# The second FFN's last product as seven half products (Strassen's scheme) instead of one full product

## The chip, the cores and the metric

One core of a Trainium2 chip runs the whole kernel. The metric is the device time of one execution in microseconds (us), as the median of several executions. The core has a matmul engine (TensorE, PE in the profile, with its weight loads as PEld), a vector engine (VectorE, DVE), an activation engine (ScalarE, ACT), a general engine (GpSimd, POOL) and a queue engine for transfers (SyncE, SP). ACT and POOL can start transfers too. Each engine takes its own instructions in order, and semaphores tie the engines together. TensorE writes its sums into PSUM, eight banks of 128 x 512 floats; everything else lives in SBUF (128 partitions) or in device memory (DRAM).

## What is computed

The reference is a residual block: a first feed-forward network (FFN), two token mixers side by side, a second FFN and a last normalisation. There are 512 tokens, 1024 model columns and 2816 hidden columns. What matters here is the end of it:

```
def swiglu(h, w1, w3, w2):
    return (jax.nn.silu(h @ w1) * (h @ w3)) @ w2

x = x + 0.5 * swiglu(rms_norm(x, ffn2_norm[l]), ffn2_w1[l], ffn2_w3[l], ffn2_w2[l])
return rms_norm(x, final_norm)
```

The "last product" of the title is the `@ w2` of the second FFN: hidden values (512 tokens x 2816) times `ffn2_w2` (2816 x 1024). Half of its result is added to x, and each token's row is then normalised by its root mean square.

## The kernel before

All large products are made to float32 accuracy from three passes in a reduced format. A float32 tile is split into a high part (a cast) and a low part (the tile less its high part); `mm3` (line 121) issues three matmuls, high x high, high x low and low x high, into one PSUM bank. `split_w` (line 111) casts on ACT (line 114) and subtracts on DVE (line 115); `split` (line 138) does the same for other tiles (lines 140 and 141).

The model columns are the partitions of the activations nearly everywhere: `xT[c]` holds columns 128c to 128c + 127 of x as 128 partitions x 512 tokens. `Norm.scale` (line 162) makes the split of the scaled x, tiles `xh` and `xl`, eight of each.

`ffn` (line 447) runs two stages. The first goes over 22 blocks j of 128 hidden columns. For each, 24 matmuls with `w1` fill the bank `pa` and 24 with `w3` the bank `pb`; `hidden` (line 452) scales both by the token's 1/rms, applies SiLU and multiplies, and splits the result into `hh[j]` and `hl[j]`. The weights come as 512 KB transfers on SP's queue into three rotating buffers `raw`, and go through `load_w`. The second stage makes the product with `w2`.

In the second FFN this second stage has two forms. Columns 0 to 511 of the result (m = 0 to 3) have model columns as the output's partitions: weights are the stationary operand, the hidden values of all tokens move, 22 x 3 matmuls for each m into the bank `pd`. The result is added to `xT[m]` (line 499), and `almost` squares it for the row sums and turns it over by four transposes (`tokens`, line 1124) into O, which has tokens as partitions. Columns 512 to 1023 are made by `last` (line 1158) with tokens as the output's partitions: 128 tokens of hidden values are stationary, 512 columns of weights move, 22 x 3 matmuls for each of four token blocks into the banks `po`. `hold` (line 1148) brings eight of the 22 weight blocks early into the tiles of `xh` and `xl` (`own`), which are free by then. Eight small matmuls (`os`, line 1163) add up the squares of the first half. The end (lines 1182 to 1191), once for each token block, adds the residual, squares, forms 1/rms, scales both halves and stores them, one on ACT's and one on SP's queue.

A scheduler puts each engine's instructions in order when the program is built, from its own estimate of times; on the chip that order is fixed.

Of the kernel before, what the change touches and what calls it, by code (L numbers as in the profile page):

```python
# [9 lines left out]
F32 = mybir.dt.float32  # L10
# [40 lines left out]
def kernel(  # L51
# [18 lines left out]
    def bank(name, pool_=None):  # L70
        pool_ = pool_ or pm
        return pool_.tile([P, T], F32, tag="b", name=name)

    def tmp(name, shape=(P, T), dt=F32, tag="t", **kw):
        return tp.tile(list(shape), dt, tag=tag, name=name, **kw)
# [42 lines left out]
    def load_w(aps, kt, n, eng=None):  # L118
        return split_w(load_raw(aps, kt, n), kt, n, eng)

    def mm3(ps, whi, wlo, xhi, xlo, first, last):
        pe.matmul(ps, whi, xhi, start=first, stop=False)  # L122
        pe.matmul(ps, whi, xlo, start=False, stop=False)  # L123
        return pe.matmul(ps, wlo, xhi, start=False, stop=last)  # L124

    def ln_act(out, in_, **kw):
        pre = act.preload_act_table_set("natural_log_exp_and_others")
# [23 lines left out]
    rtp = xctx.enter_context(tc.tile_pool(name="xr1", bufs=1, side="right"))  # L151
    xT = [rtp.tile([P, T], F32, name=f"xT{c}") for c in range(KD)]

    class Norm:


# [5 lines left out]
        def scale(s, c, eng=None, src=None):  # L162
            g = pc(s.gain + c)
            src = xT[c][:] if src is None else src
            hi = xp.tile([P, T], F32R, tag=f"xh{c}", name=f"xh{c}")
            lo = xp.tile([P, T], F32R, tag=f"xl{c}", name=f"xl{c}")
            if eng is act:
                act.activation(hi[:], src, AF.Copy, scale=g)
            else:
                dve.tensor_scalar(hi[:], src, g, None, op0=ALU.mult)  # L170
            dve.scalar_tensor_tensor(lo[:], src, g, hi[:].bitcast(F32),
                                     op0=ALU.mult, op1=ALU.subtract)
            s.hi[c], s.lo[c] = hi, lo
# [71 lines left out]
    with tc.tile_pool(name="x0", bufs=1) as x0:  # L245
# [22 lines left out]
                qpe.transpose(xps[c][:, b * P:(b + 1) * P], xin[c][:, b, :], ident[:])  # L268

        def x_hi(c):  # L270
            nrm.hi[c] = xp.tile([P, T], F32R, tag=f"xh{c}", name=f"xh{c}")
            from_ = (xps if c < 2 else xT)[c][:]
            if c % 2:
                qact.activation(nrm.hi[c][:], from_, AF.Copy, scale=pc(PAR_FFN1 + c))
            else:
                qdve.tensor_scalar(nrm.hi[c][:], from_, pc(PAR_FFN1 + c), None, op0=ALU.mult)

        def x_lo(c):
            nrm.lo[c] = xp.tile([P, T], F32R, tag=f"xl{c}", name=f"xl{c}")
            from_ = (xps if c < 2 else xT)[c][:]  # L280
            qdve.scalar_tensor_tensor(nrm.lo[c][:], from_, pc(PAR_FFN1 + c), f32(nrm.hi[c][:]),
                                      op0=ALU.mult, op1=ALU.subtract)
# [161 lines left out]
        pool.tensor_copy(ux[q1], loraw[q1, :])  # L444
        pool.tensor_tensor(ux[q1], loraw[q1, :], f32(ux[q1]), op=ALU.subtract)

    def ffn(nrm, w1, w3, w2, nxt, during=(), first=None, final=None):
        with tc.tile_pool(name="hp", bufs=1) as hp:
            hh, hl = [], []
            hp.tile([P, 96], F32, name="lead")  # L450

            def hidden(j, pa, pb):
                a = tmp("fa")
                dve.tensor_tensor(a[:], pa[:], nrm.rstd[:], op=ALU.mult)  # L454
                sa = tmp("fs")
                act.activation(sa[:], a[:], AF.Silu)
                b = tmp("fb")
                dve.tensor_tensor(b[:], pb[:], nrm.rstd[:], op=ALU.mult)  # L458
                h = tmp("fh")
                dve.tensor_tensor(h[:], b[:], sa[:], op=ALU.mult)  # L460
                hi = hp.tile([P, T], F32R, name=f"hh{j}")
                lo = hp.tile([P, T], F32R, name=f"hl{j}")
                split(hi[:], lo[:], h[:], "dve")
                hh.append(hi)
                hl.append(lo)

            summed = None
            for j in range(KF):
# [18 lines left out]
                if j in during:  # L487
                    with tc.issue_after(pin.ins), tc.issue_after(loads[-1].ins):
                        during[j]()
                hidden(j, pa, pb)  # L490
            cuts = ((0, 8), (8, 8), (16, 6))

            for m in range(KD // 2 if final else KD):
                ps = bank("pd")
                for k0, kn in cuts:
                    wh, wl = load_w([(0, w2[0][k0 * P:(k0 + kn) * P, m * P:(m + 1) * P])], kn, P)
                    for k in range(k0, k0 + kn):
                        mm3(ps[:], wh[:, k - k0, :], wl[:, k - k0, :], hh[k][:], hl[k][:], k == 0, k == KF - 1)
                dve.scalar_tensor_tensor(xT[m][:], ps[:], 0.5, xT[m][:], op0=ALU.mult, op1=ALU.add)
                nxt(m)  # L500
                if final and m == 1:
                    held = final[0]()
            if final:
                final[1](hh, hl, held)

    mix = Norm(PAR_MIX)
    xsave = dp.tile([KD, P, T], F32, name="xsave")
# [13 lines left out]
    with ExitStack() as mx:  # L521
# [567 lines left out]
        for m in range(3):  # L1089
            late_tanh(m, parted)  # L1090
        rtp = ctx.enter_context(tc.tile_pool(name="xr2", bufs=1, side="right"))
        xT[:] = [rtp.tile([P, T], F32, name=f"xS{c}") for c in range(KD)]
        for c in range(KD):
            nc.gpsimd.dma_start(xT[c][:], xsave[c])
        ms = []
# [21 lines left out]
    fg = fp.tile([P, D], F32, name="fg")  # L1117
    nc.gpsimd.dma_start(fg[:], final_norm.unsqueeze(0).broadcast_to([P, D]))
    O = fp.tile([P, NB, D], F32, name="O")
    acc = fp.tile([P, T], F32, name="facc")  # L1120
    ss, cb = [fp.tile([P, NB], F32, name=n) for n in ("ss", "cb")]
    fr = fp.tile([P, NB], F32, name="fr")

    def tokens(m, scaled=True):
        ps = pr.tile([P, NB, P], F32, tag="b", name="ot")
        for b in range(NB):
            pe.transpose(ps[:, b, :], xT[m][:, b * P:(b + 1) * P], ident[:])
        o, ms_ = O[:, :, m * P:(m + 1) * P], slice(m * P, (m + 1) * P)
        if scaled:
            dve.tensor_tensor(o, ps[:], fg[:, ms_].unsqueeze(1).broadcast_to([P, NB, P]), op=ALU.mult)  # L1130
        else:
            act.copy(o, ps[:])

    def almost(m):
        if m == 0:
            tc.keep_in_program_order(act.preload_act_table_set("natural_log_exp_and_others"))
            act.activation(acc[:], xT[m][:], AF.Square)
        else:
            sq = tmp("osq")
            act.activation(sq[:], xT[m][:], AF.Square)  # L1140
            pool.tensor_tensor(acc[:], acc[:], sq[:], op=ALU.add)
        tokens(m)


    HC = slice(D // 2, D)
    KS = 10

    def hold():
        ws = {}
        for k in range(KS, KS + KD, 2):  # L1150
            raw = load_raw([(0, ffn2_w2[0][k * P:(k + 2) * P, HC])], 2, 512)
            for i in range(2):
                parts = [xp.tile([P, T], F32R, tag=f"x{n}{k - KS + i}", name=f"own{n}{k + i}") for n in "hl"]
                split(parts[0][:], parts[1][:], raw[:, i, :])
                ws[k + i] = [t[:] for t in parts]
        return ws

    def last(hh, hl, ws):
        for m in range(KD // 2, KD):
            tokens(m, False)  # L1160
        os = bank("os", pf)
        for b in range(NB):
            pe.matmul(os[:, b:b + 1], acc[:, b * P:(b + 1) * P], ones[:, 0:1], start=True, stop=True)
        dve.tensor_scalar(cb[:], os[:, 0:NB], 1.0 / D, RMS_EPS, op0=ALU.mult, op1=ALU.add)
        ps = [bank(f"po{b}", q_) for b, q_ in zip(range(NB), (pm, pm, pf, pf))]

        def some(b, ks):
            bs = slice(b * P, (b + 1) * P)
            for k in ks:
                mm3(ps[b][:], hh[k][:, bs], hl[k][:, bs], *ws[k], k == 0, k == KF - 1)  # L1170

        for k in [*range(0, KS, 2), *range(KS + KD, KF, 2)]:
            wh, wl = load_w([(0, ffn2_w2[0][k * P:(k + 2) * P, HC])], 2, 512)
            for i in range(2):
                ws[k + i] = wh[:, i, :], wl[:, i, :]
            if k < KS:
                for b in range(NB):
                    some(b, (k, k + 1))
        for b in range(NB):
            some(b, range(KS, KF))  # L1180
            lo_, hi_, r = O[:, b, 0:D // 2], O[:, b, HC], fr[:, b:b + 1]
            dve.scalar_tensor_tensor(hi_, ps[b][:], 0.5, hi_, op0=ALU.mult, op1=ALU.add)
            junk = tmp("osq")
            act.activation(junk[:], hi_, AF.Square, accum_out=ss[:, b:b + 1])
            act.activation(r, ss[:, b:b + 1], AF.Ln, bias=cb[:, b:b + 1], scale=1.0 / D)
            act.activation(r, r, AF.Exp, scale=-0.5)
            dve.scalar_tensor_tensor(hi_, hi_, r, fg[:, HC], op0=ALU.mult, op1=ALU.mult)
            act.activation(lo_, lo_, AF.Copy, scale=r)
            bs = slice(b * P, (b + 1) * P)
            nc.scalar.dma_start(out[0, bs, 0:D // 2], lo_)  # L1190
            nc.sync.dma_start(out[0, bs, HC], hi_)

    ffn(nrm2, ffn2_w1, ffn2_w3, ffn2_w2, almost, final=(hold, last))


_INS = ['x', 'ffn1_norm', 'ffn1_w1', 'ffn1_w3', 'ffn1_w2', 'mix_norm', 'w_in', 'shift_mu',
# [21 lines left out]
```

## Time and profile before

| | |
|---|---|
| median of three executions | 1181.81 us (1181.7 to 1183.05) |
| the profiled execution | 1182.64 us, of which its span is 1180.9 us |
| granted TensorE clock, mean | 0.997 |
| transfers | 122.52 MB, mean 104 GB/s |
| POOL's (software) queue | 12.06 MB, 3.2% of 16 transfer engines |
| stage of the hidden values, second FFN | 809 to 1049 us of the span |
| its last product | 1049 to 1174 us |
| end after the last matmul | to 1180.9 us |

The span is what the profiler saw of one execution; the execution's own time is 1.7 us longer. Rows that group instructions give source line, engine, operation, the tile written and the tiles read, the shape, the count, then the busy time in us, the mean duration of one in ns, and the idle time of the engine just before them with what ended it. Rows of a timeline begin with the start in us and the duration in us. TensorE's matmuls overlap each other, so their busy times add up to more than the time that they take.

### The profile page before, as it was taken

How to read it: one execution, taken by the hardware profiler on the slowest of the kernel's cores; microseconds unless marked ns; L12 is line 12 of the kernel's file. 1: busy time of each engine (PE TensorE's matmuls, PEld its weight loads, DVE VectorE, ACT ScalarE, POOL GpSimd, SP SyncE). 2: the span in 40 equal slices, each digit the busy share in tenths (PEclk: the TensorE clock that was granted, in tenths of full speed). 3: DMA queues.
4: the chain of work that ended last, by engine and by line, in shares of the span. 5: the costliest groups of instructions: out<-in, count | busy, mean ns of one | idle time of the engine just before them, and what ended most of it. 6: DMA issues, size and time to landing. Idle time of an engine off the chain costs nothing.

```text
span 1180.9 us, 15709 instructions
## 1 busy us (share of the span) xinstructions
PE 1165.0 (99%) x6264; PEld 945.6 (80%) x6264; DVE 656.3 (56%) x981; ACT 459.5 (39%) x746; POOL 87.4 (7%) x138
## 2 busy tenths in 40 slices
PE   9999999999999999999999999999999999999997
PEld 7888888888887888887677776778888888888886
DVE  6745444543444697686767666766545445544221
ACT  6322222222224765346786765424222222223222
POOL 1200000001111111401000020121000000000100
PEclk9999999999999999999999999999999999999999
DMA  6333333323334343344123244633333333325211
GB/s 179 112 107 89 98 99 94 103 81 115 116 116 113 86 114 113 112 138 116 37 64 88 79 125 126 205 93 105 89 107 90 93 104 92 105 81 169 90 36 71
DMA packets 201783, 122.52 MB, mean 104 GB/s; under 512 B 9934, under 2 KB 191246, under 8 KB 201710
## 3 DMA queue, kind: packets, MB, share of 16 engines
q1 hardware_dynamic: 195134, 107.62, 31.6%
q0 software_dynamic: 3760, 12.06, 3.2%
q10 hardware_dynamic: 2816, 1.84, 0.5%
q8 instruction: 49, 0.80, 0.3%
q14 instruction: 24, 0.20, 0.1%
HBM read 110.82 MB, written 10.68 MB: 103 GB/s over the span
## 4 chain that ended last, share of the span: by engine, by line
PE 91%; ACT 3%; DVE 3%; DMA 2%; issue 1%; SPq 0%; ACTq 0%; DVEq 0%
PE pb L124 7%; PE pb L122 7%; PE pb L123 7%; PE pa L124 6%; PE pa L122 6%; PE pa L123 6%; PE pd L124 5%; PE pd L123 5%; PE pd L122 5%; PE pgt L122 3%; PE pgt L124 2%; PE pgt L123 2%; PE pk L123 2%; PE pk L122 2%; PE pk L124 2%; PE po L122 2%
## 5 line engine op out<-in xcount | busy, mean ns | idle before, releaser
L114 ACT CAST whi<-raw 128x1024 fp32r<-128x1024 f32 (+3 forms) x193 | 192.8, 1000 | 586.1 <-PE pa L123 177.8
L115 DVE TENSOR_TENSOR wlo<-raw,whi 128x1024 fp32r<-128x1024 f32 (+3 forms) x193 | 224.2, 1162 | 122.8 <-ACT whi L114 122.7
L124 PE MATMUL pb<-xh,wlo 128*128 128x512 f32 x344 | 133.9, 389 | 0.1
L124 PE MATMUL pa<-xh,wlo 128*128 128x512 f32 x344 | 133.9, 389 | 0.0
L122 PE MATMUL pb<-xh,whi 128*128 128x512 f32 x344 | 133.8, 389 | 0.0
L123 PE MATMUL pb<-xl,whi 128*128 128x512 f32 x344 | 133.8, 389 | 0.0
L123 PE MATMUL pa<-xl,whi 128*128 128x512 f32 x344 | 133.8, 389 | 0.0
L122 PE MATMUL pa<-xh,whi 128*128 128x512 f32 x344 | 133.8, 389 | 0.0
L458 DVE TENSOR_TENSOR fb<-pb,rstd 128x512 f32<-128x512 f32 x43 | 29.7, 691 | 139.5 <-PE pb L124 139.5
L124 PE MATMUL pd<-hh,wlo 128*128 128x512 f32 x264 | 103.1, 391 | 0.5 <-DVE wlo L115 0.5
L122 PE MATMUL pd<-hh,whi 128*128 128x512 f32 x264 | 102.8, 389 | 0.0
L123 PE MATMUL pd<-hl,whi 128*128 128x512 f32 x264 | 102.8, 389 | 0.0
L124 PEld LDWEIGHTS pb<-xh,wlo 128*128 128x128 f32 x344 | 64.5, 188 | 13.9 <-DVE wlo L241 0.6
L124 PEld LDWEIGHTS pa<-xh,wlo 128*128 128x128 f32 x344 | 64.6, 188 | 13.5
L123 PEld LDWEIGHTS pb<-xl,whi 128*128 128x128 f32 x344 | 64.6, 188 | 13.5
L123 PEld LDWEIGHTS pa<-xl,whi 128*128 128x128 f32 x344 | 64.5, 188 | 13.5
L122 PEld LDWEIGHTS pb<-xh,whi 128*128 128x128 f32 x344 | 64.6, 188 | 13.3
L122 PEld LDWEIGHTS pa<-xh,whi 128*128 128x128 f32 x344 | 64.6, 188 | 13.3
L454 DVE TENSOR_TENSOR fa<-pa,rstd 128x512 f32<-128x512 f32 x43 | 29.7, 691 | 70.3 <-PE pa L124 70.2
L124 PEld LDWEIGHTS pd<-hh,wlo 128*128 128x128 f32 x264 | 49.6, 188 | 11.1 <-DVE wlo L115 0.9
L123 PEld LDWEIGHTS pd<-hl,whi 128*128 128x128 f32 x264 | 49.6, 188 | 10.4
L122 PEld LDWEIGHTS pd<-hh,whi 128*128 128x128 f32 x264 | 49.6, 188 | 10.2
(395 smaller groups left out, 2026.0 us busy)
## 6 DMA issues: line engine op xcount, KB each, us to landing
raw<-in_ffn_w_dram SPq DMA_DIRECT2D x121, 512.0 KB
raw<-in_w_in_dram SPq DMA_DIRECT2D x40, 512.0 KB
raw<-in_ffn_w_dram SPq DMA_DIRECT2D x12, 384.0 KB
raw<-in_w_out_dram SPq DMA_DIRECT2D x8, 512.0 KB
gsave<-gs SPq DMA_DIRECT2D x9, 256.0 KB
xin<-in_x_dram SPq DMA_DIRECT2D x8, 256.0 KB
xsave<-xT POOLq DMA_DIRECT2D x8, 256.0 KB, 2.3
G<-gsave POOLq DMA_DIRECT2D x8, 256.0 KB, 3.0
```

The lines of the kernel that those rows point to most:

```text
L114: (hi_eng or act).copy(hi[:], raw[:])
L115: (eng or dve).tensor_tensor(lo[:], raw[:], hi[:].bitcast(F32), op=ALU.subtract)
L122: pe.matmul(ps, whi, xhi, start=first, stop=False)
L123: pe.matmul(ps, whi, xlo, start=False, stop=False)
L124: return pe.matmul(ps, wlo, xhi, start=False, stop=last)
L454: dve.tensor_tensor(a[:], pa[:], nrm.rstd[:], op=ALU.mult)
L458: dve.tensor_tensor(b[:], pb[:], nrm.rstd[:], op=ALU.mult)
```

## The change

The last product of the second FFN is made by Strassen's scheme in Winograd's form. The hidden columns are cut into two halves of 11 blocks, the tokens into two halves of 256, and the columns of w2 into two halves of 512. Seven products of such halves replace eight. Each has 11 k steps, two blocks of 128 tokens as stationary operands and 512 columns of weights moving, three matmuls each. Fifteen sums of halves are needed:

- On the side of the hidden values DVE makes four sums (`second`, `rest`) of float32 tiles, before the split; `hidden` therefore stores unsplit values, and `operand` splits a group of four blocks x 256 tokens at once, by ACT and DVE.
- On the side of w2, four sums are made by transfers. `load` issues for products 1, 2, 3 and 5 a transfer on POOL's queue with `accum_op=ALU.add`, which adds a quarter of w2 from DRAM onto what lies in SBUF; for products 0, 4 and 6 a plain transfer on SP's queue. A product's weights are six pieces, five of 128 x 2 x 512 floats and one half of that. Each piece has one buffer `sum[g]` and one pair of split tiles `slots[g]`. `weight` splits a piece and then issues the transfer for the next product's piece into the same buffer.
- On the side of the result, PSUM banks X, Y and Z go on collecting over several products, and DVE adds them, with factors of 0.5 and -0.5, into O (`out`).

All of O's residual is turned over beforehand: `begin`, which runs beside steps 1 to 8 of the stage of hidden values, transposes `xT[m]` into O and starts the first plain transfers into the space of `xT`. For that the tiles of `xT`, `xh` and `xl` are allotted in pairs. Row sums of squares now come from ACT over O; the eight small matmuls and `almost` go.

```
+        def load(s, n, g):
+            r, c, more = ((0, 0, 0), (0, 1, 1), (1, 1, 1), (1, 0, 1), (1, 1, 0), (0, 1, 1), (1, 0, 0))[n]
+            k0, k1 = r * KH + 2 * g, r * KH + min(2 * g + 2, KH)
+            src = s.w[k0 * P:k1 * P, c * (D // 2):(c + 1) * (D // 2)].rearrange("(k p) c -> p k c", p=P)
+            if more:
+                nc.gpsimd.dma_start(s.sum[g], src, accum_op=ALU.add)
+            else:
+                nc.sync.dma_start(s.sum[g], src)
+
+        def weight(s, n, g):
+            split(*s.slots[g], s.sum[g])
+            if n < 6:
+                s.load(n + 1, g)
...
+        def second(s, g):
+            d = s.lo[g][:, :, TH:]
+            dve.tensor_tensor(d, d, s.hi[g][:, :, TH:], op=ALU.subtract)
+            s.operand(1, g)
+
+        def rest(s, g):
+            a11, d = s.lo[g][:, :, 0:TH], s.lo[g][:, :, TH:]
+            a12, a22 = s.hi[g][:, :, 0:TH], s.hi[g][:, :, TH:]
+            dve.tensor_tensor(d, d, a11, op=ALU.subtract)
+            dve.tensor_tensor(s.e[g], a12, d, op=ALU.add)
+            dve.scalar_tensor_tensor(a11, d, -1.0, a22, op0=ALU.mult, op1=ALU.subtract)
+
+        def operand(s, n, g):
+            q, lo, hi = s.q[n % 2][g], s.lo[g], s.hi[g]
+            a, z = slice(0, TH), slice(TH, T)
+            split(q[:, 0], q[:, 1], (lo[:, :, a], lo[:, :, z], lo[:, :, z], hi[:, :, z], n == 4 and s.e[g], lo[:, :, a], hi[:, :, a])[n])
...
+            def mm(ps, n, i, k, fresh):
+                q, c = s.q[n % 2][k // 4][:, :, k % 4], slice(i * P, (i + 1) * P)
+                wh, wl = [t[:, k % 2] for t in s.slots[k // 2]]
+                mm3(ps[i][:], q[:, 0, c], q[:, 1, c], wh, wl, fresh and k == 0, k == KH - 1, n in (2, 4, 5))
...
+            put(0, 3, s.second, 2)
+            put(0, 8, s.rest, 2)
+            for n in range(6):
+                for g in range(6):
+                    put(n, 2 * g + (5 if n == 0 else 3), s.weight, n + 1, g)
+                for g in range(3):
+                    if n + 2 < 7:
+                        put(n, min(4 * g + 3, 10) + (4 if n == 0 else 0), s.operand, n + 2, g)
+            for n, ps in enumerate((X, Y, X, Z, Y, X)):
+                for k in range(KH):
+                    for i in range(2):
+                        mm(ps, n, i, k, n in (0, 1, 3))
+                    for f, *a in after.get((n, k), ()):
+                        f(*a)
+                for i in range(2):
+                    for b, cols, by in (((0, LO, 0.5),), ((2, HI, 0.5),), ((0, HI, -0.5),), ((2, LO, 0.5),),
+                                        ((0, HI, 0.5),), ((2, LO, 0.5), (2, HI, -0.5)))[n]:
+                        s.out(ps[i][:], b + i, cols, by)
```

The seventh product (into V) runs the first six k steps for both token blocks and then the other five for one block after the other, so that the first block's end can begin earlier. The end of each token block (`part`, `whole`) has the same steps as before.

More of the change, by code (lines that the diff above doesn't have):

```diff
@@ L119, in load_w, with mm3 @@
         return split_w(load_raw(aps, kt, n), kt, n, eng)
[L121 to L124, printed above, removed]
+    def mm3(ps, whi, wlo, xhi, xlo, first, last, onto=False):
+        pe.matmul(ps, whi, xhi, start=first, stop=False, skip_group_check=onto)
+        pe.matmul(ps, whi, xlo, start=False, stop=False, skip_group_check=onto)
+        return pe.matmul(ps, wlo, xhi, start=False, stop=last, skip_group_check=onto)
     def ln_act(out, in_, **kw):
@@ L152, with pair @@
     xT = [rtp.tile([P, T], F32, name=f"xT{c}") for c in range(KD)]
+    pairs = {}
+    def pair(n, c):
+        if c % 2 == 0:
+            pairs[n, c // 2] = xp.tile([P, 2, T], F32R, tag=f"x{n}{c // 2}", name=f"x{n}{c}")
+        return pairs[n, c // 2][:, c % 2]
     class Norm:
@@ L164, in scale @@
             src = xT[c][:] if src is None else src
-            hi = xp.tile([P, T], F32R, tag=f"xh{c}", name=f"xh{c}")
-            lo = xp.tile([P, T], F32R, tag=f"xl{c}", name=f"xl{c}")
+            hi, lo = pair("h", c), pair("l", c)
             if eng is act:
@@ L270, in x_hi @@
         def x_hi(c):
-            nrm.hi[c] = xp.tile([P, T], F32R, tag=f"xh{c}", name=f"xh{c}")
+            nrm.hi[c] = pair("h", c)
             from_ = (xps if c < 2 else xT)[c][:]
@@ L278, in x_lo @@
         def x_lo(c):
-            nrm.lo[c] = xp.tile([P, T], F32R, tag=f"xl{c}", name=f"xl{c}")
+            nrm.lo[c] = pair("l", c)
             from_ = (xps if c < 2 else xT)[c][:]
@@ L445, in place_params, with ffn @@
         pool.tensor_tensor(ux[q1], loraw[q1, :], f32(ux[q1]), op=ALU.subtract)
-    def ffn(nrm, w1, w3, w2, nxt, during=(), first=None, final=None):
+    def ffn(nrm, w1, w3, w2, nxt, during=(), first=None, seven=None, beside=()):
         with tc.tile_pool(name="hp", bufs=1) as hp:
@@ L450, in ffn @@
             hp.tile([P, 96], F32, name="lead")
+            if seven:
+                seven = seven(hp, w2[0])
             def hidden(j, pa, pb):
@@ L458, in hidden @@
                 dve.tensor_tensor(b[:], pb[:], nrm.rstd[:], op=ALU.mult)
+                if seven:
+                    dve.tensor_tensor(seven.hidden(j), b[:], sa[:], op=ALU.mult)
+                    seven.ready(j)
+                    return
                 h = tmp("fh")
@@ L489, in ffn @@
                         during[j]()
+                if j in beside:
+                    beside[j]()
+                if seven and j == KF - 1:
+                    seven.places()
                 hidden(j, pa, pb)
+            if seven:
+                seven.run()
+                return
             cuts = ((0, 8), (8, 8), (16, 6))
-            for m in range(KD // 2 if final else KD):
+            for m in range(KD):
                 ps = bank("pd")
@@ L500, in ffn @@
                 nxt(m)
[L501 to L504, printed above, removed]
     mix = Norm(PAR_MIX)
@@ L1091 @@
         rtp = ctx.enter_context(tc.tile_pool(name="xr2", bufs=1, side="right"))
-        xT[:] = [rtp.tile([P, T], F32, name=f"xS{c}") for c in range(KD)]
+        xS = [rtp.tile([P, 2, T], F32, name=f"xS{c}") for c in range(KD // 2)]
+        xT[:] = [xS[c // 2][:, c % 2] for c in range(KD)]
         for c in range(KD):
@@ L1119, with tokens @@
     O = fp.tile([P, NB, D], F32, name="O")
[L1120 to L1124, printed above, removed]
+    third = fp.tile([P, 2, T], F32, name="third")
+    ss, ss2, cb, fr = [fp.tile([P, NB], F32, name=n) for n in ("ss", "ss2", "cb", "fr")]
+    def tokens(m):
         ps = pr.tile([P, NB, P], F32, tag="b", name="ot")
@@ L1127, in tokens @@
             pe.transpose(ps[:, b, :], xT[m][:, b * P:(b + 1) * P], ident[:])
[L1128 to L1135, printed above, removed]
-            tc.keep_in_program_order(act.preload_act_table_set("natural_log_exp_and_others"))
[L1137 to L1142, printed above, removed]
@@ L1145 @@
[L1145 to L1151, printed above, removed]
-            for i in range(2):
[L1153 to L1191, printed above, removed]
@@ L1196, with seven @@
+    box = []
+    def seven(hp, w):
+        box.append(Seven(hp, w))
+        return box[0]
+    ffn(nrm2, ffn2_w1, ffn2_w3, ffn2_w2, None, seven=seven,
+        beside={1 + m: (lambda m=m: box[0].begin(m)) for m in range(KD)})
 _INS = ['x', 'ffn1_norm', 'ffn1_w1', 'ffn1_w3', 'ffn1_w2', 'mix_norm', 'w_in', 'shift_mu',
```

90 lines of the change are left out of this document (89 added, 1 removed).

## The prediction

> **What bounds the kernel now.** I read the shares of the page first, then the chain that ended last.
>
> ```profile
> PE 1165.0 (99%) x6264; PEld 945.6 (80%) x6264; DVE 656.3 (56%) x981; ACT 459.5 (39%) x746; POOL 87.4 (7%) x138
> PE 91%; ACT 3%; DVE 3%; DMA 2%; issue 1%; SPq 0%; ACTq 0%; DVEq 0%
> ```
>
> TensorE holds 91% of the chain, so a matmul that goes away is worth its place in the row of matmuls, if nothing else becomes late. That place is not its duration. The timeline of TensorE, as the last product begins:
>
> ```profile
> 1048.97 0.39 PE L122 MATMUL pd<-hh,whi 128*128 128x512 f32 x1
> 1049.19 0.39 PE L123 MATMUL pd<-hl,whi 128*128 128x512 f32 x1
> ...
> 1059.85 0.39 PE L122 MATMUL pd<-hh,whi 128*128 128x512 f32 x1
> ```
>
> Each lasts 0.39 us, but the next starts 0.22 to 0.23 us later. Line 122 opens each k, and 1059.85 is the opening of k = 16: 48 matmuls in 10.88 us, 0.2267 us each. The stage's other marks, from views of single tiles and of time:
>
> ```profile
> L124 PE MATMUL po<-whi,hl x56: 388/389/398, 1111.5 to 1173.8; 128*128 128x512 f32 x56
> ...
> 1117.88 0.28 PE L1163 MATMUL os<-onesr,facc 128*128 128x1 f32 x2
> 1118.02 1.07 PE L1127 MATMUL ot<-ident,xS 128*128 128x128 f32 x8
> 1118.93 0.73 PE L1163 MATMUL os<-onesr,facc 128*128 128x1 f32 x6
> 1119.52 0.47 PE L122 MATMUL po<-whi,hh 128*128 128x512 f32 x1
> ...
> 1080.48 0.50 PE L124 MATMUL pd<-hh,wlo 128*128 128x512 f32 x1 [0.47 <-DVE wlo L115]
> ```
>
> The last matmul starts at 1173.8, so the stage's place on TensorE runs from 1048.97 to about 1174.05, 125.1 us. Its 528 matmuls (4 column blocks x 22 x 3, then 22 x 4 token blocks x 3) fill 528 x 0.2267 = 119.7 us. The other 5.4 us: 32 transposes at 0.91/8 = 0.114 us, 3.65 us; eight row-sum matmuls, 1.64 - 0.91 = 0.73 us; a stall of 0.47 us; 0.5 us of small waits.
>
> **The change part by part.** *Matmuls.* Seven products of 11 k x 2 token blocks x 3 are 462 instead of 528: 66 x 0.2267 = 14.96 us less, same shape. One product is 66 too, so it lasts 14.96 us. The row-sum matmuls go, 0.73 us, and the stall and the small waits have no counterpart I can name: 1.0 us.
>
> *Transposes.* All 32 move ahead, into the stage that makes the hidden values. TensorE has no hole there:
>
> ```profile
> 814.70:1048.70 234.00, 234.00 (x1034) 193.73 (x1033) 116.69 (x149) 61.06 (x69) 0.00 (x0) 1.00 0.33 96
> ```
>
> The columns are length, PE, PEld, DVE, ACT and POOL busy, granted clock, DMA share and GB/s. So they cost 3.65 us there and save 3.65 us later: nothing. DVE has room, 117 of 234 us, and loses two instructions in each of 22 steps (rows below, 0.42 + 0.69 us). In return each half-group of hidden values is split at once, and twice a burst of five (one difference, its split, three sums, 5 x 1.22 = 6.1 us) meets the step's 2 x 1.22 + 3 x 0.69 = 4.5 us: 10.6 us in a step of 48 x 0.2267 = 10.88 us. It fits barely; I take 0 and keep 2 us as its upper end.
>
> *Splits.* Durations by form:
>
> ```profile
> L115 DVE TENSOR_TENSOR wlo<-raw,whi 128x1024 fp32r<-128x1024 f32 x58 | 70.9, 1222 | 39.8 <-ACT whi L114 39.8
> L114 ACT CAST whi<-raw 128x1024 fp32r<-128x1024 f32 x58 | 61.1, 1054 | 218.9 <-PE pa L123 91.2 <-PE pb L123 81.9 <-PE pd L123 22.5
> L141 DVE TENSOR_TENSOR hl<-fh,hh 128x512 fp32r<-128x512 f32 x22 | 15.2, 693 | 0.8
> L140 DVE CAST hh<-fh 128x512 fp32r<-128x512 f32 x22 | 9.2, 419 | 0.0
> L140 ACT CAST ownh<-raw 128x512 fp32r<-128x512 f32 x8 | 4.6, 618 | 6.2 <-DMA raw<-in_ffn_w_dram 6.2
> L115 DVE TENSOR_TENSOR wlo<-raw,whi 128x768 fp32r<-128x768 f32 x4 | 3.8, 955 | 2.4 <-ACT whi L114 2.4
> L114 ACT CAST whi<-raw 128x768 fp32r<-128x768 f32 x4 | 3.3, 836 | 12.2 <-PE pd L123 8.3 <-issue 3.9
> L1182 DVE SCALAR_TENSOR_TENSOR O<-po,O 128x512 f32<-128x512 f32 x4 | 2.8, 692 | 21.8 <-PE po L124 21.8
> ```
>
> Per product DVE subtracts five weight pieces of 128x1024 and a half one, three token operands (two of 1024, one of 768 columns) and adds two results to O: 5 x 1.22 + 0.69 + 2 x 1.22 + 0.96 + 2 x 0.69 = 11.6 us of 14.96. ACT casts the same: 5 x 1.05 + 0.62 + 2 x 1.05 + 0.84 = 8.8 us. Both are hidden while TensorE sets the pace: 0 us; without that cover DVE would be the floor at 11.6 us a product.
>
> *Weight sums.* This is the unknown. Products 1, 2, 3 and 5 take sums that 24 adding transfers on POOL's queue make in SBUF (20 of 512 KB, 4 of 256 KB); products 0, 4 and 6 load plainly on SP's. The trace has no adding transfer. Nearest are POOL's plain reads with the same 2 KB rows, and two that scatter:
>
> ```profile
> 739.40 0.54 POOL L1118 DMA_DIRECT2D fg<-in_final_norm_dram  x1 [22.70 <-PE ppj L124]
> 739.93 3.77 POOL L1094 DMA_DIRECT2D xS<-xsave  x7
> 744.00 0.55 POOL L1094 DMA_DIRECT2D xS<-xsave  x1 [0.29 <-DMA fg<-in_final_norm_dram]
> ...
> 743.40:745.40 2.00, 2.00 (x10) 1.65 (x10) 1.23 (x3) 0.73 (x2) 0.85 (x2) 1.00 1.00 335
> 745.40:747.40 2.00, 2.00 (x11) 1.65 (x10) 1.94 (x4) 1.00 (x3) 0.00 (x0) 1.00 1.05 386
> 747.40:749.40 2.00, 2.00 (x11) 1.65 (x10) 1.70 (x3) 1.14 (x2) 0.00 (x0) 1.00 1.04 366
> ...
> xsave<-xT POOLq DMA_DIRECT2D x8, 256.0 KB, 2.3
> Tall<-Td POOLq DMA_DIRECT2D x2, 128.0 KB, 6.1
> ```
>
> With the engines full (share 1.0) they moved 335 to 386 GB/s; by 366, 512 KB take 1.43 us. That is the lower bound of d, the queue's time for one adding piece. The upper is the scattering pair, 6.1 us for 128 KB, 24 us for 512 KB. An adding transfer has to read the destination as well as the source, so I take twice the plain read, d = 2.87 us: its rows are like the plain ones, far from the other's, which are 32 floats long.
>
> What d may be: the full pieces of products 1 to 3 in the queue ahead of, and with, the tightest one (the fifth of product 3, wanted at its k = 8) are 16. Count from the start of product 0. The first can go some 9 us earlier: in the changed program's order its slot's first split stands on DVE inside the last step but one. The tightest has to be split by 3 x 14.96 + 8 x 6 x 0.2267 = 55.8. Behind its bytes come the landing (the 256 KB store's 2.3 us less 0.7 us of bytes, 1.6 us), cast and subtract, 2.5 us with the hops. So -9 + 16 d + 4.1 <= 55.8: d up to 3.8 us costs nothing, 138 GB/s. At 2.87 us the queue is done 15 us early. Each microsecond beyond is worth 16 us on the path. Behind a late piece waits its cast on ACT and its subtract on DVE, and behind these, in order, the operand splits, the sums into O and the next pieces, whose transfers POOL issues only after them: nothing overtakes. Product 5's pieces start again from plain loads, 5.5 of them in some 30 us, and begin to be late at d of about 4.5 us, since product 3's last pieces then still hold the queue.
>
> The Trainium skill (Collectives: The Full Stack, Part 3) says that the addition in a DMA engine is free and a reduction runs at half the copy's rate because it reads twice, 62.3 against 32.4 GB/s. By that ratio of 1.93 d would be an estimated 2.8 us; no trace here shows it.
>
> *The end.* From the last matmul to the end of the span nothing changes in kind: sum into O, square, two tiny activations, scale, store.
>
> ```profile
> 1174.24 0.69 DVE L1182 SCALAR_TENSOR_TENSOR O<-po,O 128x512 f32<-128x512 f32 x1 [5.30 <-PE po L124]
> ...
> 1177.13 0.33 SPq L1191 DMA_DIRECT2D out_dram<-O  x1
> ```
>
> The other token block's chain is 3.1 us on DVE and ACT by these marks, under the 15 x 0.2267 = 3.4 us by which its matmuls end earlier: 0 us.
>
> **Sum.** 14.96 + 0.73 + 1.0 less 0.5 us for new small waits at six changes of product gives 16.2 us. The profiled execution took 1182.64 us (span 1180.9), 0.83 us over the median of 1181.81; 1182.64 - 16.2 = 1166.4, or 1165.6 beside the median. I say 1166.
>
> **The rivals.** *A. The adding transfers set the pace.* If d is over 3.8 us, TensorE waits 16 (d - 3.8) us; the gain is gone at d = 3.8 + 16.2/16 = 4.8 us, 109 GB/s, 3.4 times the plain read. Reading, adding and writing one row after another without overlap could do that. At a quarter of the plain rate, d = 5.73 us, it is 31 us for products 1 to 3 and about 9 us for product 5: 1166 + 40 = 1206, slower than before; at the far bound of 24 us it would be over 300 us. For it: no row shows an adding transfer, and this one also reads SBUF. Against: it needs well over the second read's price.
>
> *B. Each adding transfer pays its fixed part alone*, as the queue did not when fg and eight xS pieces went out in 5 us and filled the engines. Then d = 1.6 + 2.87 = 4.5 us and 16 x 0.7 = 11 us are lost: 1177. The Trainium skill (DMA: Bandwidth & Descriptors, Anatomy of one DMA) gives 2.0 us fixed plus the bytes at 436 GB/s; paid one by one with the bytes doubled that is an estimated 4.4 us, against overlapped starts in these rows.
>
> *C. DVE becomes the bound.* It takes 78% of a product. Were its two-input subtracts slowed 1.4 times by what POOL does for its transfers, 11.6 would become 16.2, 1.3 us over a product, six times: 1166 + 8 = 1174. Against: the 58 subtracts above average 1.22 us whatever POOL does, though POOL issues nothing beside most of them.
>
> *D. The saving doesn't come*, because the new order pays it back in small waits of TensorE: over 12 us of them, near 0.2 us at each of 66 piece changes, would leave 1180. The stage now shows one stall.
>
> **How the numbers follow.** Forecast 0.60, with its own range 1163 (no new waits at all) to 1170 (the burst's 2 us, 2 us more of waits); A 0.29 slower and 0.03 at its crossing; B 0.05; C 0.02; D 0.01. Within 0.2% (2.4 us) is what a measurement of this kernel can't tell from no change; A's crossing and D fall there, 0.04. Faster: 0.60 + 0.05 + 0.02 = 0.67. Slower: 0.29. The range goes from 1163 to 1207, A at a quarter of the plain rate; beyond it lies some 0.15 of A.
>
> **What would show it.** Right: 462 matmuls at 0.2267 us from first X to last V, about 105 us; pieces landing steadily under 3.8 us apart; casts of sums waiting for TensorE, not for DMA. Wrong: casts waiting for the sums' transfers, and holes in TensorE at the late k of product 2 and all along product 3 (A, B); or DVE without idle time there (C).

## The result and the profile after

| | before | changed |
|---|---|---|
| median | 1182.21 us (1181.7 to 1183.05, 4 runs) | 1169.54 us (1169.0 to 1169.67, 4 runs) |
| ratio, 95% interval | | 0.9891 [0.9874, 0.9908] |
| profiled execution, its span | 1182.64 us, 1180.9 us | 1169.42 us, 1167.6 us |
| granted TensorE clock, mean | 0.997 | 0.995 |

The kernel is 1.1% faster. Of the 16.2 us that were forecast, 13.2 came in the profiled executions, 12.7 in the medians. The page of the changed kernel, its shares, POOL's queue and the chain that ended last:

```profile
PE 1150.1 (98%) x6190; PEld 933.5 (80%) x6190; DVE 691.4 (59%) x996; ACT 497.1 (43%) x790; POOL 110.2 (9%) x159
...
q0 software_dynamic: 9776, 23.60, 8.8%
...
PE 93%; ACT 2%; DVE 2%; DMA 2%; issue 1%; SPq 0%; ACTq 0%; DVEq 0%
```

TensorE still holds the chain. To place the difference I cut both spans at the same two events: the first matmul of the second FFN and the start of the last matmul. The view of time windows, the kernel before (columns as in the prediction):

```profile
809.11:1173.82 364.71, 364.24 (x1626) 301.54 (x1625) 158.99 (x200) 98.46 (x122) 5.02 (x3) 1.00 0.32 94
```

and the changed kernel, whole and in pieces of 15 us through the products:

```profile
811.69:1159.91 348.22, 348.22 (x1553) 288.37 (x1551) 194.09 (x215) 136.04 (x166) 27.60 (x24) 1.00 0.47 120
...
1060.00:1075.00 15.00, 15.00 (x68) 12.44 (x67) 13.34 (x13) 7.99 (x10) 7.22 (x6) 1.00 1.12 206
1075.00:1090.00 15.00, 15.00 (x68) 12.43 (x67) 13.91 (x15) 11.56 (x13) 7.92 (x7) 1.00 1.13 206
1090.00:1105.00 15.00, 15.00 (x68) 12.43 (x67) 10.93 (x11) 8.42 (x9) 1.05 (x2) 1.00 1.08 268
1105.00:1120.00 15.00, 15.00 (x67) 12.41 (x67) 11.95 (x13) 8.53 (x9) 6.85 (x6) 1.00 0.96 188
```

The budget of the span, from these marks:

| part | before | changed | difference |
|---|---|---|---|
| start to the second FFN's first matmul | 809.11 | 811.69 | +2.58 us |
| from there to the last matmul | 364.71 | 348.22 | -16.49 us |
| from there to the end of the span | 7.08 | 7.69 | +0.61 us |
| sum | 1180.9 | 1167.6 | -13.3 us |

The stage that the change rewrites gained what the prediction said, 16.49 us against 16.2. TensorE is busy for 348.22 of 348.22 us, without a hole, though the transfer engines are full for 45 us (share 1.08 to 1.13). What is missing was lost elsewhere: 2.58 us ahead of the second FFN and 0.61 us behind its last matmul.

The larger loss lies at the end of the mixers, some 75 us before the first instruction on TensorE that the change touches (the transposes start at 829). SP's queue there, in the timeline of the changed kernel:

```profile
733.00 7.36 SPq L107 DMA_DIRECT2D raw<-in_rwkv_proj_dram  x3
740.46 0.46 SPq L1197 DMA_DIRECT2D third<-in_ffn_w_dram  x1
741.19 13.54 SPq L107 DMA_DIRECT2D raw<-in_rwkv_proj_dram  x4
```

and in that of the kernel before:

```profile
735.84 17.78 SPq L107 DMA_DIRECT2D raw<-in_rwkv_proj_dram  x6
755.65 8.62 SPq L107 DMA_DIRECT2D raw<-in_w_out_dram  x4
```

Line 1197 is the plain branch of `load`. The two pieces that `begin` starts before it go into the space of `xT`, which is freed late; this one goes into `third`, a tile of its own that waits for nothing. The order in which the program is built put it between two weight loads of the mixers' last projection, 314 us before its first cast (1054.3). TensorE at that place, changed kernel:

```profile
750.37 0.39 PE L124 MATMUL ppj<-ya,wlo 128*128 128x512 f32 x1
753.67 0.50 PE L122 MATMUL ppj<-ya,whi 128*128 128x512 f32 x1 [2.91 <-ACT whi L114]
...
755.41 0.63 PE L123 MATMUL ppj<-ya,whi 128*128 128x512 f32 x1
755.84 0.63 PE L124 MATMUL ppj<-ya,wlo 128*128 128x512 f32 x1
```

and the kernel before:

```profile
750.47 0.39 PE L124 MATMUL ppj<-ya,wlo 128*128 128x512 f32 x1
752.55 0.50 PE L122 MATMUL ppj<-ya,whi 128*128 128x512 f32 x1 [1.69 <-ACT whi L114]
```

The kernel before had a hole there already, 2.08 us from start to start; now it is 3.30 us. The cast that ends it waits for the transfer. From ACT's timeline, before and then changed:

```profile
751.88 0.62 ACT L114 CAST whi<-raw 128x512 fp32r<-128x512 f32 x1 [3.34 <-DMA raw<-in_rwkv_proj_dram]
```

```profile
753.00 0.62 ACT L114 CAST whi<-raw 128x512 fp32r<-128x512 f32 x1 [4.56 <-DMA raw<-in_rwkv_proj_dram]
```

It begins 1.12 us later; at the 364 to 398 GB/s that moved in these microseconds the 512 KB of `third` take 1.3 to 1.4 us. A second part of the price follows the hole. Windows of the changed kernel (seventh number: granted clock):

```profile
753.00:755.00 2.00, 1.33 (x4) 0.81 (x5) 1.35 (x3) 1.67 (x3) 0.00 (x0) 0.81 0.24 56
755.00:757.00 2.00, 2.00 (x6) 1.61 (x5) 1.76 (x3) 1.45 (x3) 0.00 (x0) 0.50 0.46 136
757.00:760.00 3.00, 3.00 (x13) 2.38 (x13) 1.49 (x3) 0.94 (x2) 0.00 (x0) 0.89 0.58 175
```

The clock falls to half, and the matmuls start 0.43 us apart instead of 0.23; in the kernel before it is 1.00 in each of these windows. The projection's second part, from its first matmul to the first of the next product (`pw`), takes 739.3 to 766.5, 27.2 us, where it took 739.4 to 763.8, 24.4 us.

The loss at the end, in the timeline of the changed kernel:

```profile
1159.91 0.39 PE L124 MATMUL V<-sraw,q 128*128 128x512 f32 x1
1160.33 0.69 DVE L1229 SCALAR_TENSOR_TENSOR O<-V,O 128x512 f32<-128x512 f32 x1 [0.60 <-PE V L124]
...
1163.12 0.37 ACTq L1249 DMA_DIRECT2D out_dram<-O  x1
```

and of the kernel before:

```profile
1177.10 0.37 ACTq L1190 DMA_DIRECT2D out_dram<-O  x1
```

From the last matmul to ACT's last store the two differ by less than 0.1 us (3.28 and 3.21). From that store to the end of the span it is 3.8 us before and 4.5 us now: the 0.6 us lie behind all computing.

### The profile page after: what moved, and what is told of

Its sections match the earlier page's. It is cut to its first block, busy times and chain, and to the rows that moved or that the text cites. A ratio compares the mean times of both kernels' runs of the same rounds, so it can differ in the third digit from the quotient of the medians.

```text
span 1167.6 us, 15706 instructions
## 1 busy us (share of the span) xinstructions
PE 1150.1 (98%) x6190; PEld 933.5 (80%) x6190; DVE 691.4 (59%) x996; ACT 497.1 (43%) x790; POOL 110.2 (9%) x159
## 4 chain that ended last, share of the span: by engine, by line
PE 93%; ACT 2%; DVE 2%; DMA 2%; issue 1%; SPq 0%; ACTq 0%; DVEq 0%
PE pb L124 7%; PE pb L122 7%; PE pb L123 7%; PE pa L124 7%; PE pa L122 7%; PE pa L123 7%; PE pd L123 3%; PE pd L124 3%; PE pd L122 3%; PE pgt L122 3%; PE pgt L124 2%; PE pgt L123 2%; PE pk L123 2%; PE pk L122 2%; PE pk L124 2%; PE X L124 1%
## 5 line engine op out<-in xcount | busy, mean ns | idle before, releaser
L114 ACT CAST whi<-raw 128x1024 fp32r<-128x1024 f32 (+2 forms) x174 | 173.6, 999 | 510.7 <-PE pa L123 158.4
L115 DVE TENSOR_TENSOR wlo<-raw,whi 128x1024 fp32r<-128x1024 f32 (+2 forms) x174 | 202.2, 1162 | 86.7 <-ACT whi L114 86.7
L122 PEld LDWEIGHTS pa<-xh,whi 128*128 128x128 f32 x344 | 64.6, 188 | 13.3
L122 PE MATMUL pd<-hh,whi 128*128 128x512 f32 x176 | 68.5, 389 | 0.0
L123 PE MATMUL pd<-hl,whi 128*128 128x512 f32 x176 | 68.5, 389 | 0.0
L124 PE MATMUL pd<-hh,wlo 128*128 128x512 f32 x176 | 68.5, 389 | 0.0
L122 PE MATMUL pgt<-xh,whi 128*128 128x512 f32 x128 | 53.7, 419 | 0.0
L123 PE MATMUL pgt<-xl,whi 128*128 128x512 f32 x128 | 50.4, 393 | 0.0
L124 PE MATMUL pgt<-xh,wlo 128*128 128x512 f32 x128 | 50.2, 392 | 0.0
```

The lines of the kernel that those rows point to most:

```text
L114: (hi_eng or act).copy(hi[:], raw[:])
L115: (eng or dve).tensor_tensor(lo[:], raw[:], hi[:].bitcast(F32), op=ALU.subtract)
L122: pe.matmul(ps, whi, xhi, start=first, stop=False, skip_group_check=onto)
L123: pe.matmul(ps, whi, xlo, start=False, stop=False, skip_group_check=onto)
L124: return pe.matmul(ps, wlo, xhi, start=False, stop=last, skip_group_check=onto)
```

## The experiments

Theory: the stage itself gains 16.5 us and the adding transfers are hidden; the time missing was lost because `third`'s load delays a weight piece. Rivals: the adding transfers cost something after all; the hole is the chip's spread.

### The load of `third`, held back

The plain loads that `begin` starts wait until the last weight load ahead of them in the program has been issued. With that `third`'s load goes out at 863.5 us, inside the second FFN, instead of 740.5:

```
-                s.load(0, k // 2)
+                with tc.issue_after(loads[-1].ins):
+                    s.load(0, k // 2)
```

> The plain transfer that fills `third` for product 0 is held back to step 6 of the hidden values' stage; nothing else moves. Theory (the early transfer is the loss): in the changed kernel it stands in SP's queue at 740.5 us between two transfers of rwkv_proj weights and delays the later ones by 1.1 us; TensorE's hole before `ppj` at 753.7 goes back from 3.3 us to the 2.1 us of before, the granted clock of 0.50 behind it goes back to 1.0, and the time falls by 2.7 us from 1169.5 to about 1166.9. Rival (the mixers' stage is late by chance or by the new program's layout): 1169.5, the hole stays.

Measured: 1166.54 us, ratio 0.985 [0.9835, 0.9865]; the changed kernel had 0.9891 [0.9874, 0.9908]. The hole in TensorE's timeline:

```profile
751.43 0.39 PE L124 MATMUL ppj<-ya,wlo 128*128 128x512 f32 x1
753.30 0.50 PE L122 MATMUL ppj<-ya,whi 128*128 128x512 f32 x1 [1.48 <-ACT whi L114]
```

It is 1.87 us, the clock stays at 1.00 and the stage takes 24.2 us again. Moving this one transfer out of the way gives back the loss.

### The load of fg as well

The hole that is left is older than the change. Another 512 KB transfer, fg's on POOL's queue, goes out at 739.4 just ahead of the late weight pieces (first row of the fence on POOL in the prediction), and fg isn't needed for over 300 us. So fg is no longer loaded where its tile is made; `begin` issues it behind the second norm:

```
-    nc.gpsimd.dma_start(fg[:], final_norm.unsqueeze(0).broadcast_to([P, D]))
...
+            if k == 6:
+                with tc.issue_after(nrm2.tail.ins):
+                    nc.gpsimd.dma_start(fg[:], final_norm.unsqueeze(0).broadcast_to([P, D]))
```

> As late_third, and the 512 KB transfer that fills fg is held back too, behind the last POOL sum of the squares. Theory: 512 KB fewer in front of the same rwkv_proj piece, 1.4 us at the 366 GB/s of that stretch, so that TensorE's hole there shrinks from 2.1 us to about 0.7 us: 1165.5 us. Rival (other transfers take the place at once, or the piece is late for another reason): like late_third, 1166.9 us.

Measured: 1164.57 us, ratio 0.9837 [0.9824, 0.9851]. It was run again on another chip:

> The changed kernel with the plain load of `third` behind the last weight load of its mixer and with the load of fg behind the second norm, so that neither stands between the pieces of rwkv_proj. Theory: 4.6 us under the changed kernel, of which 2.7 us were the delay that the change brought and 2 us the hole that the kernel before had already; 1164.6 us, ratio 0.984. Rival, that the earlier result was the chip's spread: within 1 us of the changed kernel, ratio 0.988.

Measured: 1164.76 us, ratio 0.9843 [0.9829, 0.9856]; the changed kernel beside it had 0.988 [0.9867, 0.9894]. The intervals do not touch: this version beats both kernels. In the window where the hole was, TensorE has none in this second run (the second number is its busy time):

```profile
751.00:753.00 2.00, 2.00 (x10) 1.68 (x9) 1.84 (x4) 1.24 (x3) 0.00 (x0) 1.00 0.44 125
```

The same move of fg, alone and in the kernel before:

> The kernel before with only its load of fg put behind the second norm. Theory: the hole of 2.1 us ahead of the rwkv_proj matmuls shrinks to under 0.5 us, and the time falls by about 2 us, ratio 0.998. Rival, that the hole comes from the rate of the weight loads alone and not from fg's transfer: hole and time unchanged, ratio 1.000.

Measured: 1180.79 us, ratio 0.9977 [0.9968, 0.9986].

```profile
751.00:753.00 2.00, 2.00 (x11) 1.65 (x9) 1.84 (x4) 1.66 (x3) 0.00 (x0) 1.00 0.38 101
```

The hole goes, the stage takes 22.2 us (740.1 to 762.3) instead of 24.4, and the rival, that the weight loads' own rate makes the hole, falls. Each 512 KB transfer among these loads costs what it makes them late; the second one costs the clock too.

### The same load added to the kernel before

If the theory holds, the load alone must slow the kernel before by 2.7 us. The first attempt gave the load an unread tile of its own, and to make room cut a pad ahead of the hidden values' tiles:

```
-            hp.tile([P, 96], F32, name="lead")
+            hp.tile([P, 72], F32, name="lead")
...
+    third = fp.tile([P, 2, T], F32, name="third")
+    nc.sync.dma_start(third[:], ffn2_w2[0][4 * P:6 * P, 0:D // 2].rearrange("(k p) c -> p k c", p=P))
```

> The kernel before with one 512 KB plain transfer more, into a tile that nobody reads, at the place in SP's queue that the changed kernel's `third` has; the output stays the reference's. Theory: 1182.2 + 2.7 = 1184.9 us, with the hole of 3.3 us and the clock of 0.50 of the changed kernel. Rival: 1182.2 us, no difference.

Measured: 1193.13 us, ratio 1.0076 [1.0063, 1.0089], a loss of some 9 us. The hole and the clock's fall were there (stage 743.3 to 770.4, 27.1 us), but the first FFN had already ended later, so more than the load had changed. The second attempt writes into O, which is not yet in use, and moves no tile:

```
+    nc.sync.dma_start(O[:, 0].rearrange("p (k c) -> p k c", k=2),
+                      ffn2_w2[0][4 * P:6 * P, 0:D // 2].rearrange("(k p) c -> p k c", p=P))
```

> The kernel before, all tiles where they were, with one 512 KB plain transfer more at the place in SP's queue that the changed kernel's `third` has; it goes into O, which is written anew later, so the output stays the reference's. Theory (that transfer alone makes the hole and the drop of the clock): 2.7 us over before, ratio 1.0023; the stage from the first to the last matmul of `ppj<-ya` lasts 27.1 us instead of 24.4 us. Rival (the 9 us of before_third came from the transfer): ratio 1.0076.

Measured: 1185.42 us, ratio 1.0019 [1.001, 1.0028], 2.7 us more. In TensorE's timeline:

```profile
750.74 0.39 PE L124 MATMUL ppj<-ya,wlo 128*128 128x512 f32 x1
754.09 0.50 PE L122 MATMUL ppj<-ya,whi 128*128 128x512 f32 x1 [2.95 <-ACT whi L114]
```

The hole of 3.35 us is that of the changed kernel, and the clock falls with it (0.56 from 755 to 757). None of Strassen's scheme is in this kernel: the load alone makes the loss. The rest of the first attempt's loss, by the pad alone:

> The kernel before with only the lead pad of the tile of hh and hl cut from 96 to 72 floats, which shifts these tiles by 96 bytes in each partition, and no transfer. Theory: the part of the earlier miss that the transfer does not explain (about 6.5 us) is the shift; ratio 1.0055, pd matmuls of 397 ns instead of 389. Rival: the shift does nothing, ratio 1.000, pd matmuls of 389 ns.

Measured: 1190.51 us, ratio 1.0058 [1.0044, 1.0072]. The view of tile `pd`, kernel before:

```profile
L122 PE MATMUL pd<-hh,whi x264: 387/389/402, 251.3 to 1110.4; 128*128 128x512 f32 x132
```

and with the shorter pad:

```profile
L122 PE MATMUL pd<-hh,whi x264: 392/397/411, 250.8 to 1116.7; 128*128 128x512 f32 x132
```

The median rises from 389 to 397 ns with nothing changed but where the tiles lie. The first 48 matmuls of the second FFN's `pd` take 11.24 us (1053.48 to 1064.72) against 10.88, so 0.0075 us each; for 1056 in the two FFNs that is 7.9 us, near the measured 7.0. So the first attempt's miss had two causes, and its 9 us say nothing against the theory.

### The adding transfers without the addition

```
-                nc.gpsimd.dma_start(s.sum[g], src, accum_op=ALU.add)
+                nc.gpsimd.dma_start(s.sum[g], src)
```

> The changed kernel with its 24 adding transfers made plain ones of the same size on the same queue (the sums of w2 are left out, so products 1, 2, 3 and 5 use unsummed weights). Theory (the adding transfers are hidden): the same 1169.5 us within 0.5 us, the queue's share of the transfer engines falls from 8.8% to about 6.0% (22 pieces of 1.43 us instead of 2.95 us). Rival (adding costs small waits or slows the splits): faster by over 1 us.

Measured: 1170.73 us, ratio 0.9885 [0.9871, 0.9898], the same ratio as the changed kernel's three (0.9891, 0.9886 and 0.988). Its page:

```profile
q0 software_dynamic: 6960, 23.60, 6.4%
```

The same bytes take 6.4% instead of 8.8% of the 16 engines' span, yet no time is gained. That the addition is hidden is shown here by leaving it out, and not only inferred from a full TensorE.

### How much slower they might be

Behind each adding transfer, on the same queue, comes a plain copy between two places of DRAM, of half a piece's size (first run) or a whole one's (second run):

```
-                nc.gpsimd.dma_start(s.sum[g], src, accum_op=ALU.add)
+                adding = nc.gpsimd.dma_start(s.sum[g], src, accum_op=ALU.add)
+                idle = dp.tile([P, k1 - k0, 256], F32, name=f"idle{n}{g}")
+                with tc.issue_after(adding.ins):
+                    nc.gpsimd.dma_start(idle[:], src[:, :, 0:256])
```

> The changed kernel with 256 KB of plain copying from DRAM to DRAM behind each of the 24 adding transfers, on the same queue (128 KB behind a half piece). Theory (the queue's time per piece costs nothing up to 3.8 us, then 16 us for each): 2.95 us measured per piece plus 0.72 us at 366 GB/s is 3.67 us, so 1169.5 us as the changed kernel; if the copy's rate is half, 4.4 us and 10 us more, 1180. Rival (the transfer engines are full already at 2.95 us, so more is paid at once): 22 x 0.72 = 16 us or more, 1185 us.

> As extra256 with 512 KB each: 2.95 + 1.43 = 4.38 us a piece. Theory: 16 x (4.38 - 3.8) = 9 us more, 1179 us; at half the copy's rate 5.8 us a piece, 32 us and 9 us for product 5, 1210 us. Rival: 22 x 1.43 = 31 us already at the full rate, 1201 us. In either kernel TensorE's holes should lie at the late k of products 2 and 3.

Measured: 1172.57 us, ratio 0.9915 [0.9899, 0.9932], and 1184.31 us, ratio 1.0011 [1.0001, 1.002]. Both are slower than the theory on record said (1169.5 and 1179). From 1062 to 1090 us only POOL's queue moves data (SP issues at 1055.8, then not before 1091.3) and the transfer engines are full. The changed kernel, then the half-size and the full-size copies, in the view of time windows (last two numbers: share and GB/s):

```profile
1062.00:1090.00 28.00, 28.00 (x125) 23.22 (x124) 25.50 (x27) 17.55 (x20) 15.14 (x13) 1.00 1.13 206
```

```profile
1062.00:1090.00 28.00, 28.00 (x125) 23.20 (x124) 22.44 (x23) 14.28 (x16) 18.74 (x20) 1.00 1.11 247
```

```profile
1062.00:1090.00 28.00, 27.93 (x123) 22.58 (x122) 20.19 (x21) 13.52 (x15) 16.78 (x18) 1.00 1.10 275
```

512 KB at 206 GB/s take 2.55 us; with 256 KB of copy behind each, at 247 GB/s, a piece takes 3.18 us, and with 512 KB, at 275 GB/s, 3.81 us. This is the d of the prediction. The half-size copies' first holes in TensorE's timeline:

```profile
1112.62 0.50 PE L122 MATMUL Z<-swhi,q 128*128 128x512 f32 x1 [0.98 <-ACT swhi L140]
1113.88 0.50 PE L123 MATMUL Z<-swlo,q 128*128 128x512 f32 x1 [0.76 <-DVE swlo L141]
```

They stand at the late k of product 3, the place that the prediction named as the tightest. The full-size copies:

```profile
1096.32 0.39 PE L124 MATMUL X<-swhi,q 128*128 128x512 f32 x1
1101.92 1.22 PE L122 MATMUL X<-swhi,q 128*128 128x512 f32 x2 [5.22 <-ACT swhi L140]
...
1120.00 0.40 PE L124 MATMUL Z<-swhi,q 128*128 128x512 f32 x1
1124.05 1.22 PE L122 MATMUL Z<-swhi,q 128*128 128x512 f32 x2 [3.65 <-ACT swhi L140]
```

Here product 2 waits too, and each hole brings the half clock behind it. Windows of the same kernel:

```profile
1102.00:1104.00 2.00, 2.00 (x5) 1.47 (x6) 2.00 (x2) 0.82 (x1) 0.77 (x2) 0.50 1.08 289
1104.00:1106.00 2.00, 2.00 (x6) 1.52 (x6) 0.27 (x1) 0.72 (x1) 0.26 (x1) 0.50 1.06 352
```

The order of some instructions on the engines shifted a little in this kernel, so the last microsecond of its time should not be read.

### The changed kernel beside the others

> The changed kernel itself, to stand beside the others on one chip: ratio 0.989 to before, with the hole of 3.3 us before `ppj` in the mixers' stage.

Measured: 1169.18 us, ratio 0.9886 [0.9872, 0.9899].

> The changed kernel again, beside the others of this chip. Ratio to the kernel before 0.9886 as measured so far (0.9874 to 0.9908), 1169 us.

Measured: 1169.87 us, ratio 0.988 [0.9867, 0.9894]. The gain is the same in all three measurements.

## Why the prediction was right, and where it fell short

**Direction and mechanism: right.** The second FFN gained 16.49 us where the sum said 16.2. The terms that the traces show are 66 matmuls at 0.2267 us (14.96), the row sums (0.73) and the stall (0.47), together 16.16.

**New small waits, 0.5 us: not there.** TensorE has no wait in the new products, so the six changes of product cost nothing. (From the first X, 1044.99, to the last V, 1159.91, it is 114.9 us and not 105, because six of product 0's matmuls run among those of the last hidden step.)

**Transposes and the burst on DVE: 0, right.** With 32 transposes more and its splits in bursts, the stage of the hidden values leaves TensorE no hole; DVE is busy 110.7 of its first 233.3 us.

**The adding transfers, d = 2.87 us: right in kind, 11% high.** At 206 GB/s with full engines d was 2.55 us, 1.78 times the plain 1.43 us. The packets' time gives the same ratio. POOL's queue took 0.088 x 1167.6 = 102.7 us of the 16 engines, against 0.032 x 1180.9 = 37.8 before; the 64.9 us more, over 22 full pieces (20, and four halves), are 2.95 us each. The same pieces without the addition took 0.064 x 1169.0 = 74.8 us, so 1.68 us each: 1.75 times. (2.95 us is more than 2.55 because in these windows the packets' times add up to 1.13 of the engines' time.) The Trainium skill (Collectives: The Full Stack, Part 3) puts a reduction at half the copy's rate, because it reads twice; both ratios here lie somewhat under its 1.93. Rival A at a quarter of the rate is out, and so is rival B, 4.5 us with each fixed part paid alone: the engines were full from piece to piece.

**"d up to 3.8 us costs nothing": too generous.** At 3.18 us the kernel was already 3.4 us slower than the changed kernel beside it (the intervals of the two just touch), at 3.81 us 15.1 us slower. A straight line through these two, an estimate since there are only two, has a slope of 11.7 / 0.63 = 19 us for each microsecond, near the prediction's 16, and meets zero at 3.0 us. So A's crossing, where the whole gain is gone, lay at about 3.8 us, not at 4.8. The undisturbed trace agrees. The fifth piece of product 3 is cast at 1100.86, its subtract ends at 1103.17, and its first matmul starts at 1111.17: 8.0 us of slack, where the prediction's sum gives 19.9 us for d = 2.55. Over 16 pieces these 8.0 us are 0.5 us each, so waits would begin at an estimated 3.05 us. Two things in POOL's and SP's timelines show where the sum was wrong: the queue did not run from the first transfer on,

```profile
1043.29 1.27 POOL L1195 DMA_DIRECT2D xS<-in_ffn_w_dram  x1 [233.34 <-issue]
1049.04 0.90 POOL L1195 DMA_DIRECT2D sum<-in_ffn_w_dram  x1 [4.48 <-DVE sraw L141]
1055.67 1.19 POOL L1195 DMA_DIRECT2D xS<-in_ffn_w_dram  x1 [5.73 <-DVE sxl L141]
```

so that one and a half pieces went out in its first 12 us; and from 1091.3 on product 4's plain loads on SP's queue share the engines with product 3's last pieces. How the missing 12 us divide between the two was not tried. The mark "casts of sums waiting for TensorE, not for DMA" was wrong too. The view of waits for the changed kernel, second FFN's end:

```profile
ACT swhi L140 <- DMA sxh<-in_ffn_w_dram: 9.0, 3, 4.8
```

Casts do wait for the sums' transfers, up to 4.8 us, only not long enough for TensorE to notice.

**"One product is 66 too", C and D: as said.** DVE is busy for at most 13.9 us of 15 in a window and TensorE waits for it nowhere; its subtracts of 128x1024 average 1.22 us beside POOL's issues, as before.

**The step that failed is the list of what the change moves.** The prediction said of the plain transfers only that "products 0, 4 and 6 load plainly on SP's", and the sum gave them no term. It did not ask where in SP's queue they would stand. The load of `third` waits for no data, so it went ahead to the mixers' weight loads and cost 2.7 us there: 1.2 us of longer hole (3.30 less 2.08), the rest at the half clock. Both directions show it: held back, the projection's second part came from 27.2 to 24.2 us and the median from 1169.54 to 1166.54; put alone into the kernel before, the load cost 2.7 us.

**"From the last matmul to the end of the span nothing changes in kind": off by 0.6 us.** The time lies between the last store's issue and the end of the span. The stores of the two last token blocks are now issued 3.4 us apart instead of 8.2, which may be why; no run tried it, and it stays open. It is not chance, and not the addition: in the five traces of kernels with the old end this time is 3.77 to 3.86 us, in the nine with the new end 4.43 to 4.52, `plain_sums` among them with 4.45.

With 2.6 us and 0.6 us put in, 1166.4 becomes 1169.6; the profiled execution took 1169.42. The prediction's own range went to 1170, but its upper part was kept for the burst and for new waits, which cost nothing. That it also covered the loss in the mixers and at the end was luck.

## What to carry to other kernels

A transfer whose destination is free from the start has no place of its own: look up where it lands in its queue and what stands behind it there, however far that is from its use, and tie it to an instruction near its use if those loads are on the path. When a product is remade to need fewer matmuls, the saving is the count times their spacing, provided each new producer keeps its piece under the pace that the tightest consumer sets, and a late piece costs more than its delay. An experiment that adds a tile moves others; a matmul row whose mean duration has changed gives that away.

## What the runs showed of the hardware

*The clock falls after a hole of about 3 us.* Holes of 1.87 us (`third` held back), 1.98 us (shorter pad) and 2.08 us (kernel before) left the granted clock at 1.00; holes of 3.19 us (half-size copies), 3.30, 3.35, 4.05 and 5.60 us were each followed by some 3 us or more in which it fell to between 0.50 and 0.56 and matmuls started 0.43 us apart. At this place no run has a hole between 2.08 and 3.19 us. The Trainium skill (TensorE: Matmul & The Clock Gate, Part 1) tells of half the clock after an idle window of about 3.4 us that runs freely, and 426.7 ns from start to start at this size; the traces agree with the spacing, and show the fall after a wait of 2.81 us by the profile's count (the hole of 3.19 us), under that window.

*An adding transfer costs POOL's queue more to issue.* For one 512 KB adding transfer POOL is held about 1.2 us (the four into `third`: 1.20 to 1.28); the same four without the addition (`plain_sums`) hold it 0.72 to 0.73 us.

*Where tiles lie can change the matmul rate.* A shift of `hh` and `hl` by 96 bytes in each partition made the matmuls that read them 2% longer (389 to 397 ns) and their spacing 3% wider, 7.0 us over the kernel; the matmuls into `pa`, which don't read them, kept 389 ns. What about the place decides was not tried.
